# Retention of the first half in two blocks with a state between them, the state handed on as float32

## The chip, the cores and the metric

The kernel runs on one core of one Trainium2 chip. The metric is the device time of one execution in microseconds (us); before the change it is 1715.69 us, the median of three runs (1715.61, 1715.69 and 1717.03). The engines are named as in the profile: PE (TensorE, matmuls; PEld are its weight loads), DVE (VectorE), ACT (ScalarE), POOL (GpSimd) and SP (SyncE, which issues the DMAs).

## The reference

The reference is a trunk of two layers on 1024 tokens of width 1024. Layer 0 is retention with 4 heads (q and k of width 256, v of width 512), a norm of each head's output and a SiLU gate; layer 1 is stick-breaking attention with 8 heads on shared keys and values. Both are followed by an output projection, an RMS norm and the residual. What the change touches is retention:

```python
# o_t = sum_{s<=t} gamma_h^(t-s) (q_t . k_s) v_s
def step(state, inp):
    qc, kc, vc = inp
    scores = jnp.einsum('bhid,bhjd->bhij', qc, kc) * intra_decay
    o = jnp.einsum('bhij,bhje->bhie', scores, vc)
    o = o + jnp.einsum('bhid,bhde->bhie', qc * q_decay[None, :, :, None], state)
    state = state * chunk_decay[None, :, None, None] + jnp.einsum(
        'bhjd,bhje->bhde', kc * k_decay[None, :, :, None], vc)
    return state, o
```

The sum over earlier tokens can be cut anywhere: what lies in the same block goes through scores, what lies before it through a state of 256 x 512 numbers for each head.

## The kernel before, in words

The work has four phases: retention on the first 512 tokens (t=0), on the second 512 (t=1), then attention on each half. In a retention phase the four heads u = 0 to 3 follow each other. Each head has a projection of q and k (`qk`), one of v and the gate (`vg`), and an output projection (`out`, 16 chunks of 12 matmuls each), and the heads overlap: while the projections of head u run, `merge` strews in the steps of head u − 1 and u: the scores, the mixing of v (`mix`), the gate, and the norms of the neighbouring phase. A product is made in three matmuls (`mm3`: high with high at L415, high with low at L416, low with high at L417), because every float32 operand is kept as a high and a low part. `split` makes these: ACT writes the high part (L577), DVE the rest (L578).

Matmul results stand in PSUM banks under the tags "z" (scores, transposes, small sums), "o" (outputs of mix and states), "ma" and "mb" (projections). In the traces they are the tiles pz, po, pma and pmb; whl are split weights, xh split inputs, qk split q and k (and the last head's gated output), oT the gated output of other heads, ko split states, sc split scores, v split v, sgn normed outputs, wraw raw weights from memory.

At t=0 a head's scores are four steps `score(jb)`, the key block jb against all queries from there on (512, 384, 256 and 128 columns), and four `kt(tb)`, which transpose k. `o(ib)` then sums the score blocks 0 to ib times v. The state that the second half needs is made by two `state_out` steps, each a sum over all four token blocks; they lie beside the output projection (`L.give`), are scaled by a power of gamma, split, and written to memory as high and low parts (512 KB each). At t=1 `state_in` loads those parts as they are, and `o(ib)` takes the state's product and all score blocks.

The order around this is not written out by hand alone. `run` fixes which steps are strewn beside which projection (`nmix` says how many steps of mix lie beside `vg`; `held` is the output projection of the head before, of which a part goes in front of `vg` of the last head and the rest behind it). Then `arrange` takes the whole program and gives every engine's queue a new order by estimated costs, bank releases and due times. Within a queue the order is then fixed, so an instruction whose input isn't ready holds up everything behind it on that engine.

The last phase ends in `finish`: sums of squares, the mean over channels by matmuls with one column (L1454, L1455), a power on POOL (L1458), its broadcast by PE (L1464), the multiply by DVE (L1470) and the addition of the residual (L1471), then the DMA to the output.

Of the kernel before, what the change touches and what calls it, by code (L numbers as in the profile page):

```python
# [21 lines left out]
NH = 4  # L22
# [78 lines left out]
def arrange(nc, tc, tag_of, bufs, banks, turns):  # L101
# [4 lines left out]
    for ins in nc.cur_bb.bb.instructions:  # L106
# [12 lines left out]
        for name, m in reads:  # L119
            s.before |= {o.k for o, n, w in last[name] if w and n & m}  # L120
            s.behind |= set([o.k for o, n, w in last[name] if not w and n & m and o.eng == s.eng][-1:])
# [187 lines left out]
def trunk(ctx, tc, xT, wts, gains, trig, ident_in, cols, out):  # L309
# [26 lines left out]
    def DRAM(name, dt):  # L336
        return dr.tile([128, 1024], dt, tag=name, name=name)
# [15 lines left out]
    def hl(tag):  # L353
        return S(tag, [2, 512], F32R)
# [231 lines left out]

    st_d = [[DRAM(f"st{h}{d}", F32R) for d in range(2)] for h in range(NH)]
    y_d = [[dr.tile([128, 512], F32, tag=f"y{t}{c}", name=f"y{t}{c}") for c in range(8)] for t in range(2)]
# [137 lines left out]
    class AHead:  # L726
# [142 lines left out]
        def scores(self):  # L869
# [25 lines left out]

            st = [lambda jb=jb: score(jb) for jb in range(4)]
            if self.t == 0:
                st += [lambda tb=tb: kt(tb) for tb in range(4)]
            return st

        def mix(self):
# [3 lines left out]

            def state_out(d):
                p = PS("o")
                for tb in range(4):
                    n, kn, v = slice(128 * d, 128 * d + 128), self.kn[tb], self.v[tb]
                    mm3(p[:], kn[:, 0, n], kn[:, 1, n], v[:, 0, :], v[:, 1, :], tb == 0, tb == 3)  # L910
                s = hl("ko")
                gg = GAMMA[h] ** HT
                A_.activation(s[:, 0, :], p[:], AF.Copy, scale=gg)
                V.scalar_tensor_tensor(s[:, 1, :], p[:], gg, f32(s[:, 0, :]), ALU.mult, ALU.subtract)
                dma(st_d[h][d][:], flat(s))

            def state_in():
                for d in range(2):
                    s = hl("ko")
                    dma(flat(s), st_d[h][d][:])  # L920
                    self.state.append(s)

            def o(ib):
                p = PS("o")
                il = slice(128 * ib, 128 * ib + 128)
                for d, s in enumerate(self.state):
                    mm3(p[:], q[d][:, 0, il], q[d][:, 1, il], s[:, 0, :], s[:, 1, :], d == 0, False)
                for jb in range(ib + 1):
                    n = slice(128 * (ib - jb), 128 * (ib - jb) + 128)
                    sc, v = self.sc[jb], self.v[jb]  # L930
                    mm3(p[:], sc[:, 0, n], sc[:, 1, n], v[:, 0, :], v[:, 1, :], not self.state and jb == 0, jb == ib)
                bs, mv = S("small", [6]), S("small", [2])
# [480 lines left out]
    def finish(t, P, y_d):  # L1413
# [36 lines left out]
        def col(th):  # L1450
            p = PS("z")
            for b in range(2):
                o = 256 * th + 128 * b
                MM(p[:, b:b + 1], acc[:, o:o + 128], mean[:, 0:1], start=True, stop=False)  # L1454
                MM(p[:, b:b + 1], box["q"][:, 128 * b:128 * b + 128], mean[:, 0:1], start=False, stop=True)  # L1455
            ms, r = S("small", [2]), S("col", [4])
            V.tensor_scalar(ms[:], p[:, 0:2], EPS, None, ALU.add)
            G.tensor_tensor(r[:, 0:2], ms[:], mhalf[:, 0:2], ALU.pow)  # L1458
            box["r"] = r
# [6 lines left out]
        def write(th, k):  # L1466
            tl = slice(256 * th, 256 * th + 256)
            yy = f[:, 2 * k:2 * k + 2, tl]
            h = hs[k][:].rearrange("p (c t) -> p c t", c=2)[:, :, tl]
            V.tensor_tensor(yy, yy, box["row"][:, :256].unsqueeze(1).broadcast_to([128, 2, 256]), ALU.mult)  # L1470
            (G if th == 0 or k == 0 else V).tensor_tensor(yy, yy, h, ALU.add)  # L1471
            dma(out[256 * k:256 * k + 256, HT * t + 256 * th:HT * t + 256 * th + 256].rearrange("(c p) t -> p c t", c=2), yy)
# [20 lines left out]
    def run():  # L1493
# [12 lines left out]
        for ip, (kind, t) in enumerate(phases):  # L1506
# [5 lines left out]
            for u in range(4):  # L1512
                ring[:] = rings(kind, t, u)
                if kind == "A":
# [143 lines left out]
```

## Time and profile before

| | us |
|---|---|
| median of three runs | 1715.69 |
| the profiled execution | 1716.91 |
| its span | 1714.8 |
| PE busy | 1700.1 |
| DVE busy | 1308.4 |
| ACT busy | 880.9 |
| POOL busy | 142.8 |

The profile shows one execution. Its span runs from the first to the last instruction on the chip; the 2.1 us between it and the execution's time lie around it. "Busy" is the time in which at least one instruction was under way. Matmuls are pipelined, one starts before the last has ended, so their durations must not be added up: the distance between the starts of two is what one costs. A wait is shown behind an instruction in square brackets, with the time that its engine stood idle and the instruction that released it.

### The profile page before, as it was taken

To read this page: it belongs to the slowest core of one execution; us is meant where nothing else is said; L and a number is where in the kernel's file an instruction comes from. 1 tells how busy PE (TensorE), PEld (TensorE's weight loads), DVE (VectorE), ACT (ScalarE), POOL (GpSimd) and SP (SyncE) were. 2 spreads that over 40 slices of the span, in tenths; PEclk is the share of its full clock that TensorE was granted. 3 is DMA by queue.
4 is the path that set the end of the run, shared out by engine and by line. 5 is a ranking of instruction groups with operands and counts; after the bars stand their busy time and mean duration, and the time that the engine had idled before them with its cause. 6 is when DMAs were issued, how large, how long until landed. Compare 5 with 4: busy or idle time off the path is not lost.

```text
span 1714.8 us, 23975 instructions
## 1 busy us (share of the span) xinstructions
PE 1700.1 (99%) x8057; PEld 1419.0 (83%) x8057; DVE 1308.4 (76%) x2213; ACT 880.9 (51%) x1646; POOL 142.8 (8%) x275
## 2 busy tenths in 40 slices
PE   9999999999999999999999999999999999999997
PEld 7888888888888888878888888888888888888887
DVE  8856868889867978688888778667887756656865
ACT  6435536555545535355655544544674445445643
POOL 0000101010010000101010100000001001001001
PEclk9999999999999999999999999999999999999999
DMA  5236475668545676376896999667883763463523
GB/s 187 98 105 203 148 236 185 203 193 271 187 146 176 225 240 209 98 256 209 291 320 198 332 314 308 209 209 257 280 292 111 252 225 101 160 219 99 162 95 125
DMA packets 182250, 348.78 MB, mean 203 GB/s; under 512 B 20208, under 2 KB 24432, under 8 KB 182128
## 3 DMA queue, kind: packets, MB, share of 16 engines
q1 hardware_dynamic: 182128, 347.26, 61.0%
q8 instruction: 63, 1.03, 0.2%
q14 instruction: 59, 0.48, 0.1%
HBM read 273.78 MB, written 73.40 MB: 202 GB/s over the span
## 4 chain that ended last, share of the span: by engine, by line
PE 99%; DMA 0%; DVE 0%; ACT 0%; issue 0%; SPq 0%; POOL 0%; DVEq 0%
PE pmb L415 13%; PE pmb L417 13%; PE pmb L416 13%; PE pma L415 12%; PE pma L417 12%; PE pma L416 12%; PE po L417 5%; PE po L416 5%; PE po L415 5%; PE pz L1355 2%; PE pz L417 2%; PE pz L416 2%; PE pz L415 2%; PE pz L983 1%; PE pz L551 0%; DMA S<-in_xT_dram 0%
## 5 line engine op out<-in xcount | busy, mean ns | idle before, releaser
L577 ACT ACTIVATE whl<-wraw 128x512 fp32r<-128x512 f32 x323 | 190.8, 625 | 203.4 <-PE pmb L417 80.4
L578 DVE TENSOR_TENSOR whl<-wraw,whl 128x512 fp32r<-128x512 f32 x323 | 214.3, 686 | 64.3 <-ACT whl L577 63.1
L415 PE MATMUL pma<-xh,whl 128*128 128x512 f32 x384 | 153.1, 399 | 0.0
L415 PE MATMUL pmb<-xh,whl 128*128 128x512 f32 x384 | 152.4, 397 | 0.0
L417 PE MATMUL pma<-xh,whl 128*128 128x512 f32 x384 | 150.1, 391 | 0.0
L417 PE MATMUL pmb<-xh,whl 128*128 128x512 f32 x384 | 150.0, 391 | 0.0
L416 PE MATMUL pma<-xh,whl 128*128 128x512 f32 x384 | 149.9, 390 | 0.0
L416 PE MATMUL pmb<-xh,whl 128*128 128x512 f32 x384 | 149.6, 390 | 0.0
L1325 DVE TENSOR_TENSOR_SCAN sgn<-sgn 128x384 f32<-128x384 f32 (+4 forms) x64 | 86.5, 1354 | 27.7 <-POOL sgn L1323 27.7
L580 ACT ACTIVATE whl<-wraw,gn 128x256 fp32r<-128x256 f32 (+1 forms) x144 | 80.4, 600 | 50.0 <-PE pmb L417 32.4
L577 ACT ACTIVATE AT<-pz 128x512 fp32r<-128x512 f32 (+1 forms) x96 | 46.3, 487 | 108.0 <-PE pz L1355 105.9
L1322 POOL TENSOR_SCALAR_AFFINE_SELECT A<-A 128x128 f32<-128x128 f32 x64 | 33.1, 516 | 775.1 <-ACT A L1317 775.1
L578 DVE TENSOR_TENSOR AT<-pz,AT 128x512 fp32r<-128x512 f32 (+1 forms) x96 | 52.9, 555 | 57.6 <-ACT AT L577 57.1
L581 DVE SCALAR_TENSOR_TENSOR whl<-wraw,gn,whl 128x256 fp32r<-128x256 f32 (+1 forms) x144 | 82.0, 601 | 17.1 <-ACT whl L580 16.5
L415 PE MATMUL pmb<-oT,whl 128*128 128x512 f32 x240 | 94.9, 396 | 0.0
L417 PE MATMUL pmb<-oT,whl 128*128 128x512 f32 x240 | 93.8, 391 | 0.0
L416 PE MATMUL pmb<-oT,whl 128*128 128x512 f32 x240 | 93.7, 391 | 0.0
L577 ACT ACTIVATE whl<-S 128x512 fp32r<-128x512 f32 x104 | 63.0, 628 | 48.1 <-PE pmb L417 12.5
L417 PEld LDWEIGHTS pmb<-xh,whl 128*128 128x128 f32 x384 | 72.1, 188 | 15.8
L417 PEld LDWEIGHTS pma<-xh,whl 128*128 128x128 f32 x384 | 72.1, 188 | 15.6
L416 PEld LDWEIGHTS pmb<-xh,whl 128*128 128x128 f32 x384 | 72.2, 188 | 13.5
L415 PEld LDWEIGHTS pmb<-xh,whl 128*128 128x128 f32 x384 | 72.2, 188 | 13.4
(389 smaller groups left out, 4614.0 us busy)
## 6 DMA issues: line engine op xcount, KB each, us to landing
wraw<-in_wts_dram SPq DMA_DIRECT2D x522, 256.0 KB, 3.6
y<-f SPq DMA_DIRECT2D x120, 256.0 KB, 3.2
f<-y SPq DMA_DIRECT2D x88, 256.0 KB, 4.1
S<-in_wts_dram SPq DMA_DIRECT2D x44, 256.0 KB, 4.1
vo<-in_wts_dram SPq DMA_DIRECT2D x42, 256.0 KB, 4.3
ko<-in_wts_dram SPq DMA_DIRECT2D x40, 256.0 KB, 4.4
T<-AT SPq DMA_DIRECT2D x32, 256.0 KB, 4.7
sc<-T SPq DMA_DIRECT2D x16, 512.0 KB, 5.1
```

The costliest lines, as they stand in the source:

```text
L415: MM(p, lh, rh, start=start, stop=False, **kw)
L416: MM(p, lh, rl, start=False, stop=False, **kw)
L417: MM(p, ll, rh, start=False, stop=stop, **kw)
L577: A_.activation(dst[0], src, AF.Copy)
L578: V.tensor_tensor(dst[1], src, f32(dst[0]), ALU.subtract)
L580: A_.activation(dst[0], src, AF.Copy, scale=scale)
L581: V.scalar_tensor_tensor(dst[1], src, scale, f32(dst[0]), ALU.mult, ALU.subtract)
L983: nc.tensor.transpose(pt[:, 128 * e:128 * e + 128], on[:, 128 * e:128 * e + 128], ident[:])
L1322: first = G.affine_select(a[:, dg], a[:, dg], [[-1, 128]], ALU.is_gt, 0.0, base=0, channel_multiplier=1)
L1325: V.tensor_tensor_scan(n[:, :W][:, ::-1], n[:, :W][:, ::-1], n[:, :W][:, ::-1], 1.0, ALU.mult, ALU.bypass)
L1355: nc.tensor.transpose(p[:, 128 * tb:128 * tb + 128], self.A[hh][tb][:, c0:c0 + 128], ident[:])
```

## The change

Retention at t=0 is cut into two blocks of 256 tokens. For each head:

- the scores are two steps `pair(c)`, each with 256 and 128 columns in one bank, behind the transposes of k;
- `o(0)` and `o(1)` take the blocks 0 and 1, `o(2)` and `o(3)` take the state of the first block and the blocks 2 and 3;
- two `carry(d)` steps behind `o(0)` make the state: the first six matmuls sum the first 256 tokens, that sum is split (the state for `o(2)` and `o(3)`), and six more add the next 256 tokens in the same bank. ACT scales the result into a float32 tile "sc2", of which there is one buffer, and it is written as it is (256 KB). `state_out` and its place beside the output projection are gone;
- at t=1 `state_in` loads the float32 state into the ring of raw weights and splits it there.

Beside that, five steps of mix in place of two lie beside `vg` at t=0. Of the last head's held output projection eight chunks in place of four stand in front of `vg`, in banks of both tags. `arrange` now also puts a read of a PSUM tile behind earlier reads of it by another engine. In `finish` the four mean matmuls are reordered, for the second 256 tokens ACT copies half of two residual tiles into PSUM banks, and the additions are shared otherwise: POOL adds three of four for the first 256 tokens (four before) and two of four for the second (one before), DVE the others.

```diff
-            s.before |= {o.k for o, n, w in last[name] if w and n & m}
+            s.before |= {o.k for o, n, w in last[name] if n & m and (w or name in banks and o.eng != s.eng)}
...
-    st_d = [[DRAM(f"st{h}{d}", F32R) for d in range(2)] for h in range(NH)]
+    st_d = [[dr.tile([128, 512], F32, tag=f"st{h}{d}", name=f"st{h}{d}") for d in range(2)] for h in range(NH)]
...
-            st = [lambda jb=jb: score(jb) for jb in range(4)]
+            def pair(c):
+                p = PS("z")
+                for jb, at, w in ((2 * c, 0, 256), (2 * c + 1, 256, 128)):
+                    i0 = 256 * c + 256 - w
+                    jl, il = slice(128 * jb, 128 * jb + 128), slice(i0, i0 + w)
+                    for d in range(2):
+                        mm3(p[:, at:at + w], k[d][:, 0, jl], k[d][:, 1, jl], q[d][:, 0, il], q[d][:, 1, il],
+                            at == 0 and d == 0, at > 0 and d == 1, goes_on=True)
+                s = S(f"sc{c}", [2, 384], F32R)
+                split((s[:, 0, :], s[:, 1, :]), p[:, :384])
...
             if self.t == 0:
-                st += [lambda tb=tb: kt(tb) for tb in range(4)]
-            return st
+                return [lambda tb=tb: kt(tb) for tb in range(4)] + [lambda c=c: pair(c) for c in range(2)]
+            return [lambda jb=jb: score(jb) for jb in range(4)]
...
-            def state_out(d):
-                p = PS("o")
-                for tb in range(4):
-                    n, kn, v = slice(128 * d, 128 * d + 128), self.kn[tb], self.v[tb]
-                    mm3(p[:], kn[:, 0, n], kn[:, 1, n], v[:, 0, :], v[:, 1, :], tb == 0, tb == 3)
-                s = hl("ko")
-                gg = GAMMA[h] ** HT
-                A_.activation(s[:, 0, :], p[:], AF.Copy, scale=gg)
-                V.scalar_tensor_tensor(s[:, 1, :], p[:], gg, f32(s[:, 0, :]), ALU.mult, ALU.subtract)
-                dma(st_d[h][d][:], flat(s))
+            def carry(d):
+                p, gg, n = PS("o"), GAMMA[h] ** HT, slice(128 * d, 128 * d + 128)
+                for half in range(2):
+                    for tb in (2 * half, 2 * half + 1):
+                        kn, v = self.kn[tb], self.v[tb]
+                        mm3(p[:], kn[:, 0, n], kn[:, 1, n], v[:, 0, :], v[:, 1, :], tb == 0, tb % 2 == 1, goes_on=half == 1)
+                    if half == 0:
+                        s = hl("ko")
+                        split((s[:, 0, :], s[:, 1, :]), p[:])
+                        self.state.append(s)
+                f = S("sc2", [512])
+                A_.activation(f[:], p[:], AF.Copy, scale=gg)
+                dma(st_d[h][d][:], f[:])
...
-                    s = hl("ko")
-                    dma(flat(s), st_d[h][d][:])
+                    raw, s = raw_w(), hl("ko")
+                    dma(raw, st_d[h][d][:])
+                    split((s[:, 0, :], s[:, 1, :]), raw)
...
-                for d, s in enumerate(self.state):
+                j0 = 0 if self.t else ib // 2 * 2
+                far = self.state if self.t or j0 else []
+                for d, s in enumerate(far):
...
-                for jb in range(ib + 1):
+                for jb in range(j0, ib + 1):
...
-            if self.t == 0:
-                self.give = [lambda d=d: state_out(d) for d in range(2)]
-                return os
             self.give = []
-            return [state_in] + os
+            if self.t:
+                return [state_in] + os
+            return os[:1] + [lambda d=d: carry(d) for d in range(2)] + os[1:]
...
-            (G if th == 0 or k == 0 else V).tensor_tensor(yy, yy, h, ALU.add)
+            if th and k > 1:
+                h = box[k][:].rearrange("p (c t) -> p c t", c=2)
+            (G if k < (2 if th else 3) else V).tensor_tensor(yy, yy, h, ALU.add)
...
-                        held = last.out(yd, None, None if u < 3 else ("ma",) * 4)
-                        go(held if u < 3 else held[:4],
+                        held = last.out(yd)
+                        go(held if u < 3 else held[:8],
...
-                        held = held[4:]
-                    H.nmix = 3 if t else 2
+                        held = held[8:]
+                    H.nmix = 3 if t else 5
```

In the rows below, a row is an instruction of one engine's queue, with the engines and queues that it waits for in brackets (Activation is ACT).

The first place is PE's queue where `vg` of the last head at t=1 begins. The L569 pair sums up rows for the next phase's norm, pz<-qk are the head's scores, pma and pmb<-oT the held chunks, pma<-whl,xh the projection. Before:

```order
L417 MATMUL pma_7094<-oT_6787,whl_7011 128x512
L569 MATMUL pz_7111<-sgn_7067,onesr 128x512 [waits DVE_49,PE_49]
L569 MATMUL pz_7111<-sgn_7067,onesr 128x512 [waits DVE_49]
L415 MATMUL pz_7187<-qk_6988 128x512 [waits PE_49,Activation_49]
L416 MATMUL pz_7187<-qk_6988 128x512 [waits DVE_49]
```

And now:

```order
L417 MATMUL pmb_7139<-oT_6789,whl_7069 128x512
L569 MATMUL pz_7156<-sgn_7095,onesr 128x512 [waits DVE_49,PE_49]
L569 MATMUL pz_7156<-sgn_7095,onesr 128x512 [waits DVE_49]
L415 MATMUL pma_7170<-whl_7121,xh_3856 128x512 [waits DVE_49,Activation_49]
L416 MATMUL pma_7170<-whl_7121,xh_3856 128x512
```

The first score matmul of the head now stands 36 matmuls behind the pair, and the projection's first product stands in its place.

The second place is PE's queue at the end of the last head's gate at t=1: pz<-ident are the transposes of the gate (L983 before, L1003 now), pmb<-oT the end of the held chunks, pma<-qk the first chunk of this head's own output projection, which reads what the transposes leave. Before, the transposes and the first reader, with 24 matmuls between them:

```order
L417 MATMUL pma_7734<-oT_6787,whl_7624 128x512
L983 MATMUL pz_7760<-ident,sgn_7672 128x128 [waits DVE_49,PE_49]
L983 MATMUL pz_7760<-ident,sgn_7672 128x128 x3
L415 MATMUL pmb_7767<-oT_6787,whl_7725 128x512
```

```order
L417 MATMUL pmb_7797<-oT_6787,whl_7725 128x512
L415 MATMUL pma_7815<-qk_7578,whl_7788 128x512 [waits Activation_49]
L416 MATMUL pma_7815<-qk_7578,whl_7788 128x512 [waits DVE_49]
```

And now:

```order
L416 MATMUL pmb_7805<-oT_6789,whl_7713 128x512
L1003 MATMUL pz_7765<-ident,sgn_7705 128x128 [waits DVE_49,PE_49]
L1003 MATMUL pz_7765<-ident,sgn_7705 128x128 x3
L417 MATMUL pmb_7805<-oT_6789,whl_7713 128x512
L415 MATMUL pma_7823<-qk_7629,whl_7796 128x512 [waits Activation_49]
L416 MATMUL pma_7823<-qk_7629,whl_7796 128x512 [waits DVE_49]
```

One matmul is left between the transposes and the reader.

The third place is PE's queue in the first head's first carry at t=0. po_942 is the carry's bank, v_403 and vo_734 its first operands, pmb and pma the projection beside it. Before, the state's twelve matmuls stood together, with no wait among them, beside the output projection. Now:

```order
L417 MATMUL po_942<-v_406,vo_765 128x512
L415 MATMUL pmb_898<-xh_434,whl_832 128x512
L416 MATMUL pmb_898<-xh_434,whl_832 128x512
L417 MATMUL pmb_898<-xh_434,whl_832 128x512
L415 MATMUL pmb_899<-xh_434,whl_832 128x512
L416 MATMUL pmb_899<-xh_434,whl_832 128x512
L417 MATMUL pmb_899<-xh_434,whl_832 128x512
L415 MATMUL pma_896<-xh_463,whl_927 128x512
L416 MATMUL pma_896<-xh_463,whl_927 128x512
L415 MATMUL po_942<-v_427,vo_799 128x512 [waits DVE_49]
```

Eight matmuls of the projection stand between the two halves, and the second half waits for DVE, which must have read the first half's sums.

More of the change, by code (lines that the diff above doesn't have):

```diff
@@ L894, in score @@
                 self.sc.append(s)
-            st = [lambda jb=jb: score(jb) for jb in range(4)]
+            def pair(c):
[8 more added lines that the diff above has]
+                split((s[:, 0, :], s[:, 1, :]), p[:, :384])
+                for at in (0, 256):
+                    G.affine_select(s[:, :, at:at + 128], f32(s[:, :, at:at + 128]), [[0, 2], [1, 128]], ALU.is_ge, 0.0,
+                                    base=0, channel_multiplier=-1)
+                self.sc += [s[:, :, 0:256], s[:, :, 256:384]]
             if self.t == 0:
-                st += [lambda tb=tb: kt(tb) for tb in range(4)]
-            return st
+                return [lambda tb=tb: kt(tb) for tb in range(4)] + [lambda c=c: pair(c) for c in range(2)]
+            return [lambda jb=jb: score(jb) for jb in range(4)]
         def mix(self):
@@ L925, in o @@
                 il = slice(128 * ib, 128 * ib + 128)
-                for d, s in enumerate(self.state):
+                j0 = 0 if self.t else ib // 2 * 2
+                far = self.state if self.t or j0 else []
+                for d, s in enumerate(far):
                     mm3(p[:], q[d][:, 0, il], q[d][:, 1, il], s[:, 0, :], s[:, 1, :], d == 0, False)
-                for jb in range(ib + 1):
+                for jb in range(j0, ib + 1):
                     n = slice(128 * (ib - jb), 128 * (ib - jb) + 128)
                     sc, v = self.sc[jb], self.v[jb]
-                    mm3(p[:], sc[:, 0, n], sc[:, 1, n], v[:, 0, :], v[:, 1, :], not self.state and jb == 0, jb == ib)
+                    mm3(p[:], sc[:, 0, n], sc[:, 1, n], v[:, 0, :], v[:, 1, :], not far and jb == j0, jb == ib)
                 bs, mv = S("small", [6]), S("small", [2])
@@ L1453, in col @@
                 o = 256 * th + 128 * b
-                MM(p[:, b:b + 1], acc[:, o:o + 128], mean[:, 0:1], start=True, stop=False)
-                MM(p[:, b:b + 1], box["q"][:, 128 * b:128 * b + 128], mean[:, 0:1], start=False, stop=True)
+                MM(p[:, b:b + 1], acc[:, o:o + 128], mean[:, 0:1], start=b == 0, stop=False, skip_group_check=True)
+            for b in range(2):
+                MM(p[:, b:b + 1], box["q"][:, 128 * b:128 * b + 128], mean[:, 0:1], start=False, stop=b == 1, skip_group_check=True)
+            if th:
+                for k in (2, 3):
+                    box[k] = PS("ma")
+                    A_.activation(box[k][:].rearrange("p (c t) -> p c t", c=2),
+                                  hs[k][:].rearrange("p (c t) -> p c t", c=2)[:, :, 256:512], AF.Copy)
             ms, r = S("small", [2]), S("col", [4])
```

## The prediction

> **What bounds the kernel now.** I read the page's first lines, then the chain that ended last, then PE's own waits, then the busy time by stretches.
>
> ```profile
> span 1714.8 us, 23975 instructions
> PE 1700.1 (99%) x8057; PEld 1419.0 (83%) x8057; DVE 1308.4 (76%) x2213; ACT 880.9 (51%) x1646; POOL 142.8 (8%) x275
> PE 99%; DMA 0%; DVE 0%; ACT 0%; issue 0%; SPq 0%; POOL 0%; DVEq 0%
> ...
> PE pz L415 <- ACT qk L577: 1.8, 1, 1.8
> PE pz L1464 <- POOL col L1458: 1.0, 1, 1.0
> PE pz L1454 <- DVE acc L1447: 0.9, 1, 0.9
> ...
> 385.83:428.70 42.87, 42.87 (x197) 35.49 (x196) 41.44 (x75) 22.15 (x40) 0.00 (x0) 1.00 0.82 271
> 728.79:771.66 42.87, 41.05 (x180) 33.74 (x179) 37.41 (x62) 24.00 (x44) 1.94 (x3) 0.96 0.78 257
> 1671.93:1714.80 42.87, 33.09 (x255) 31.76 (x253) 23.24 (x49) 16.32 (x36) 8.27 (x7) 0.91 0.38 125
> ```
>
> PE is busy 99% of the span and carries 99% of the chain, so the time is the sum of PE's paces, plus its few waits, plus the end. A saving on another engine counts only where PE waits. There are three such places here: one wait of 1.8 us for a split (in 728.79 to 771.66, where PE is busy 41.05 of 42.87 us and the granted clock is 0.96), two of about 1 us at the end, and the end itself, which is work of DVE and POOL. The other danger is a stretch like 385.83 to 428.70: there DVE is busy 41.44 of 42.87 us while PE is full.
>
> The profiled run took 1716.91 us, 2.1 over its span, and 1.2 over the median of 1715.69 us. I sum against 1716.91 and keep the 1.2 for the low end of the range.
>
> **Part 1: narrower scores.** The matmuls of each o(ib) keep their number and width (3, 6, 9, 12), and the state's matmuls were there before, 24 a head. What goes is width in the scores of four heads: per head 6 matmuls each of 512, 384, 256 and 128 columns become twice 6 of 256 and 6 of 128. Durations overlap, so a matmul's price is the distance between starts.
>
> ```profile
> 64.22 0.39 PE L415 MATMUL pz<-qk 128*128 128x512 f32 x1
> 65.58 0.39 PE L415 MATMUL pma<-whl,xh 128*128 128x512 f32 x1
> 66.94 0.33 PE L415 MATMUL pz<-qk 128*128 128x384 f32 x1
> 68.00 0.39 PE L415 MATMUL pma<-whl,xh 128*128 128x512 f32 x1
> 69.39 0.28 PE L415 MATMUL pz<-qk 128*128 128x256 f32 x1
> 70.10 0.39 PE L415 MATMUL pmb<-whl,xh 128*128 128x512 f32 x1
> 71.48 0.22 PE L415 MATMUL pz<-qk 128*128 128x128 f32 x1
> 72.10 0.44 PE L415 MATMUL pmb<-whl,xh 128*128 128x512 f32 x1
> 72.39 0.40 PE L416 MATMUL pmb<-whl,xh 128*128 128x512 f32 x1
> ```
>
> Each block is timed to the first start behind it: 1.36 us (65.58 − 64.22), 1.06, 0.71 and 0.62. The wide matmul behind the narrowest ones took 0.29 (72.39 − 72.10) in place of 0.227 (1.36/6), so 0.06 more. A head's scores cost 3.81 us; afterwards 2 × (0.71 + 0.62 + 0.06) = 2.78. Times four heads this is **−4.1 us**, all on PE, so all on the path. The pace follows width down to 0.10 us a matmul in these rows (0.62/6), so nothing else caps it; I allow 0.4 either way.
>
> **Part 2: the wait at 730.** Where the last head of the second half begins, its first score matmul waited for the split of q and k (L577).
>
> ```profile
> 729.88 0.63 PE L569 MATMUL pz<-sgn,onesr 128*128 128x512 f32 x2
> 732.33 0.50 PE L415 MATMUL pz<-qk 128*128 128x512 f32 x1 [1.82 <-ACT qk L577]
> 735.77 0.63 PE L415 MATMUL pma<-whl,xh 128*128 128x512 f32 x1
> 736.20 0.63 PE L416 MATMUL pma<-whl,xh 128*128 128x512 f32 x1
> 737.45 0.40 PE L416 MATMUL pma<-whl,xh 128*128 128x512 f32 x1
> 737.68 0.39 PE L417 MATMUL pma<-whl,xh 128*128 128x512 f32 x1
> ```
>
> Two matmuls of 0.227 from 729.88 end their pace at 730.33, so the start at 732.33 is 2.00 us late. Then the clock is low: 735.77 to 736.20 is 0.43 us for a matmul that takes 0.23 at 737.45. From 732.33 to 737.45 stand 6 matmuls of 512, 5 of 384 and 4 of 512; at normal pace that is 10 × 0.227 + 5 × 0.177 = 3.15 us, and it took 5.12, so 1.97 more. Together 4.0 us. Afterwards eight held chunks of the out-projection go first instead of four, and 36 matmuls (8.2 us) of the value and gate projection stand between the pair of L569 and the first score. That covers the 1.8 us four times over, so I take **−4.0 us**. What becomes next late is the split of the first weights of that projection. They are loaded by the same ring, and the added four chunks (48 matmuls, 10.9 us) give their splits room; I count 1 to 4 us to spare for the first three. Bounds: −4.0, and 0 if the wait only moves to those weights.
>
> [...]
>
> **Part 3: the end.** The last writes are DVE's multiplies (L1470), then adds (L1471).
>
> ```profile
> 1707.03 2.48 DVE L1470 TENSOR_TENSOR oT<-oT,pz 128x512 f32<-128x512 f32 x4 [1.63 <-PE pz L1464]
> 1707.86 1.27 POOL L1471 TENSOR_TENSOR oT<-oT,A 128x512 f32<-128x512 f32 x1 [1.67 <-DVE oT L1470]
> 1709.43 1.89 DVE L1471 TENSOR_TENSOR oT<-oT,A 128x512 f32<-128x512 f32 x3
> ```
>
> DVE adds three times at 0.63 us; afterwards twice, and POOL's second add (1.27) follows its first at 1709.13 and ends at 1710.4, before DVE's second (1710.7). So **−0.6 us**. The two copies on ACT fall while the mean and its power are worked out, where ACT has nothing else. The first half's add that moves to DVE costs 0.6 if it delays the last sums, and the reordered mean matmuls can give back as much: bounds 0 to −1.2.
>
> **Part 4: the new wait at the last head's gate.** This is the price of the eight chunks. Only eight remain to cover the gate of head 3 in the second half, so its last transposes stand one matmul ahead of the first reader of qk; 24 stood there before.
>
> ```profile
> 800.84 0.60 PE L983 MATMUL pz<-ident,sgn 128*128 128x128 f32 x4
> 801.20 0.48 PE L415 MATMUL pmb<-oT,whl 128*128 128x512 f32 x1
> 801.64 0.58 ACT L577 ACTIVATE qk<-pz 128x512 fp32r<-128x512 f32 x1
> 802.25 0.69 DVE L578 TENSOR_TENSOR qk<-pz,qk 128x512 fp32r<-128x512 f32 x1
> 806.76 0.39 PE L415 MATMUL pma<-qk,whl 128*128 128x512 f32 x1
> ```
>
> The split ends at 802.94 (802.25 + 0.69). With one matmul behind the transposes and one of the reader's that needs only ACT's part, PE would be through at 801.20 + 0.46 = 801.66: a gap of 1.3 us. ACT was late by about 0.2 for a weight split of 801.10, which need not stand there. I take **+1.1 us**, bounds 0 (if the transposes come through early) and 1.3, and 2.0 more if the clock drops as after 732.33. In the first half's last gate six matmuls (1.4 us) remain, about as long as the split; there I count nothing, and 0.2 if it is late.
>
> **Part 5: the carries.** Each of eight carries now stops half way: its second six matmuls overwrite the sums that ACT and DVE are splitting. Between the halves stand 8 to 12 other matmuls, 1.8 to 2.7 us, and a prompt split takes 0.2 (801.64 after the transposes' end at 801.44) + 0.60 + 0.68 = 1.5. So I count nothing; the cover is 0.3 to 1.2 us thick, and each place costs what the queue of ACT or DVE holds beyond it. The scaled copy into the one "sc2" buffer makes the second carry's copy wait for the first one's DMA, 20 matmuls (4.5 us) later, and its bank is wanted another 30 (6.8 us) after that. The DMA now carries 256 KB; 512 KB took 5.5 us in the median, so nothing is counted either.
>
> ```profile
> st<-ko SPq DMA_DIRECT2D x8, 512.0 KB, 5.5
> ```
>
> The split of the loaded state (eight operations of 0.6 us on ACT and eight on DVE) lies beside full PE work, far ahead of its readers.
>
> **Sum.** 1716.91 − 4.1 − 4.0 − 0.6 + 1.1 = **1709.3 us**, 6.4 under the median, 0.37%.
>
> **The rivals.**
>
> Slower: the splits between the carry's halves come late. Before, the two halves of the same kind of split stood far apart on their engines.
>
> ```profile
> 325.71 0.60 ACT L913 ACTIVATE ko<-po 128x512 fp32r<-128x512 f32 x1 [0.99 <-PE po L417]
> 326.58 0.68 DVE L914 SCALAR_TENSOR_TENSOR ko<-po,ko 128x512 fp32r<-128x512 f32 x1
> 401.22 0.60 ACT L913 ACTIVATE ko<-po 128x512 fp32r<-128x512 f32 x1 [1.72 <-PE po L417]
> 420.67 0.68 DVE L914 SCALAR_TENSOR_TENSOR ko<-po,ko 128x512 fp32r<-128x512 f32 x1
> ```
>
> At 325.71 DVE followed ACT by 0.87 us, at 401.22 by 19.5. With that lag in the last head's two carries PE would wait about 2 × (19.5 + 0.9 − 2.7) = 35 us: 1744. It decides from 1.4 us a place (11 us over eight places eats the gains of 7.6 and 3.4 more). Against it: nobody waited for the split then, so DVE took it last; now it stands in DVE's queue right behind the sums it reads, and by DVE's paces I find it done 0.3 to 1 us early. Chance 4%.
>
> DVE bounds the passage from the first to the second half. Held chunks and state matmuls (10.9 us of PE) leave the stretch before head 0 of the second half, where DVE was full, and DVE's work there stays.
>
> ```profile
> 415.12 0.42 DVE L636 TENSOR_TENSOR f<-S 128x256 f32<-128x256 f32 x1
> 415.46 0.68 DVE L517 TENSOR_TENSOR f<-pma,f 128x512 f32<-128x512 f32 x1
> 416.06 0.41 DVE L637 TENSOR_TENSOR f<-S,f 128x256 f32<-128x256 f32 x1
> ```
>
> DVE's pace is 0.34 us for 256 columns and 0.60 for 512. From the last o(3) to the weights of that head's third unit I count 41 wide operations, 11 half-wide, 4 of the norm (0.66 each) and 0.8 us of small ones: 31.9 us, plus 1.2 of waiting at the gate. PE has 147 matmuls and four sets of transposes there, 35.0 us. It holds by 1.9 us. If it fails it costs 2 to 6 us with the clock: 1711.3 to 1715.3. Chance 9%, half of it above 1712.3.
>
> The clock drops after part 4's wait: +2.0, 1711.3, chance 10%. The row at 732.33 speaks for it, its wait was longer.
>
> The slow stretch at 732 was not the wait's, and only 2.0 of part 2 come back: 1711.3. For it: two other waits at the end were not followed by wide matmuls, so the rows show it once only. Chance 8%. [...]
>
> The wait at 730 moves whole to the first weights: 1713.3, chance 4%.
>
> **How the numbers follow.** The forecast has 65%. About 0.2% (3.4 us, so 1712.3) is what a measurement of this kernel can tell from no change. Faster: 65 + 10 + 8 + half of 9 is 87%. Same: 5 + 4 is 9%. Slower: 4%. The low end is 1709.3 − 1.2 (the median against the profiled run) − 1.1 (no wait at the gate) − 0.6 (the end) − 0.4 (the scores) = 1706.0; the high end is the wait that moves whole, 1713.3. Left out are the slower rival and the upper half of DVE's, some 9%.
>
> **What would show it.** Scores of 256 and 128 columns in one bank, 1.39 us a pair; no wait of PE for qk behind L569, and a granted clock of 1.00 there; a wait of about 1 us of the matmul pma<-qk on the split behind the last gate; two adds of DVE at the end, 0.6 us earlier. Wrong would be: waits of po on DVE inside the carries, PE below full in the passage from the first to the second half, or a new low clock anywhere.

## The result, and the profile after

The changed kernel takes 1709.84 us in the median of six runs (1708.51 to 1710.98), the kernel before 1715.65 (1715.2 to 1717.25, six runs). The ratio is 0.9963, with a 95% interval from 0.9953 to 0.9973: 5.8 us faster, 0.37%. The prediction was 1709.3 us, in a range from 1706.0 to 1713.3.

The profiled run took 1709.47 us with a span of 1707.8. First lines of the page, PE's waits (who waited for whom: total, times, longest), and three stretches of it (length, then busy time of PE, PEld, DVE, ACT and POOL, then granted clock, DMA share, GB/s):

```profile
span 1707.8 us, 23993 instructions
PE 1694.7 (99%) x8057; PEld 1414.8 (83%) x8057; DVE 1309.3 (77%) x2213; ACT 888.2 (52%) x1656; POOL 141.9 (8%) x275
...
PE pz L1490 <- POOL col L1484: 1.0, 1, 1.0
PE pmb L416 <- DVE whl L578: 0.7, 1, 0.7
PE pma L415 <- ACT qk L577: 0.5, 1, 0.5
PE pz L1474 <- DVE acc L1467: 0.3, 1, 0.3
PE pma L416 <- DVE qk L578: 0.2, 1, 0.2
...
384.25:426.95 42.70, 42.70 (x198) 35.27 (x197) 40.22 (x75) 21.90 (x39) 1.01 (x3) 1.00 0.76 259
725.82:768.51 42.69, 42.69 (x196) 35.58 (x195) 38.45 (x65) 25.01 (x45) 5.14 (x2) 1.00 0.87 289
768.51:811.21 42.70, 42.01 (x192) 34.35 (x191) 38.13 (x67) 22.02 (x40) 8.54 (x14) 1.00 0.64 206
```

PE is still busy 99% of the span. The wait for qk of 1.8 us is gone, and in the stretch 725.82 to 768.51 PE is full at a granted clock of 1.00. New is a wait for qk in 768.51 to 811.21 (0.5 and 0.2 us, the reader behind the last gate) and one for whl of 0.7. The passage to the second half (384.25 to 426.95) is full: DVE did not become the bound there. The wait of the mean matmuls fell from 0.9 to 0.3 us, and a wait of 1.2 us for oT in the first 10 us is not there. That one is not the change's: in three more profiles of the kernel before (below) such waits are 1.5, 0.3 and 1.2 us together.

The scores of one pair, in PE's timeline of the changed kernel (start, length, instruction):

```profile
74.52 0.28 PE L415 MATMUL pz<-qk 128*128 128x256 f32 x1
75.23 0.22 PE L415 MATMUL pz<-qk 128*128 128x128 f32 x1
75.85 0.45 PE L415 MATMUL pmb<-whl,xh 128*128 128x512 f32 x1
76.14 0.39 PE L416 MATMUL pmb<-whl,xh 128*128 128x512 f32 x1
```

From 74.52 to 75.85 are 1.33 us, and the wide matmul behind takes 0.29 in place of 0.23: 1.39 us a pair, the predicted figure to the digit, so 2.78 us a head in place of 3.81. Counted in the same way over all four heads, the scores take 15.2 us of PE before and 11.1 after.

The gate of the last head, PE, ACT and DVE of the changed kernel:

```profile
797.84 0.60 PE L1003 MATMUL pz<-ident,sgn 128*128 128x128 f32 x4
798.20 0.47 PE L417 MATMUL pmb<-oT,whl 128*128 128x512 f32 x1
798.48 0.60 ACT L577 ACTIVATE qk<-pz 128x512 fp32r<-128x512 f32 x1 [1.81 <-PE pz L1003]
799.11 0.69 DVE L578 TENSOR_TENSOR qk<-pz,qk 128x512 fp32r<-128x512 f32 x1
799.13 0.49 PE L415 MATMUL pma<-qk,whl 128*128 128x512 f32 x1 [0.46 <-ACT qk L577]
799.85 0.50 PE L416 MATMUL pma<-qk,whl 128*128 128x512 f32 x1 [0.23 <-DVE qk L578]
```

The reader starts 0.70 us later than a matmul's pace behind 798.20, and its second matmul 0.49 later still: 1.2 us, against 1.1 predicted. The end:

```profile
1697.34 0.61 PE L1476 MATMUL pz<-mean,f 128*128 128x1 f32 x4
1699.73 2.48 DVE L1496 TENSOR_TENSOR oT<-oT,pz 128x512 f32<-128x512 f32 x4 [1.59 <-PE pz L1490]
1700.56 2.50 POOL L1499 TENSOR_TENSOR oT<-oT,A 128x512 f32<-128x512 f32 x2 [1.63 <-DVE oT L1496]
1702.12 1.28 DVE L1499 TENSOR_TENSOR oT<-oT,pma 128x512 f32<-128x512 f32 x2
```

DVE adds twice and is done at 1703.40, POOL at 1703.06, as forecast.

The two profiled spans differ by 7.0 us. From the starts of PE's matmuls: scores −4.1; the wait at 730 and the slow matmuls behind it −4.0; the gate +1.2; a later split of whl near 560 +0.7; waits in the first 20 us about −0.8; and the end, from the start of the last projection matmul to the span's end, −0.1 (11.84 before, 11.77 after). Together −7.1.

### The profile page after: what moved, and what is told of

Same layout as the page of the kernel before. It is cut to its first block, busy times and chain, and to the rows that moved or that the text cites. A ratio compares the mean times of both kernels' runs of the same rounds, so it can differ in the third digit from the quotient of the medians.

```text
span 1707.8 us, 23993 instructions
## 1 busy us (share of the span) xinstructions
PE 1694.7 (99%) x8057; PEld 1414.8 (83%) x8057; DVE 1309.3 (77%) x2213; ACT 888.2 (52%) x1656; POOL 141.9 (8%) x275
## 4 chain that ended last, share of the span: by engine, by line
PE 96%; DVE 2%; DMA 1%; issue 0%; ACT 0%; SPq 0%; POOL 0%; DVEq 0%
PE pmb L415 13%; PE pmb L417 12%; PE pmb L416 12%; PE pma L415 12%; PE pma L416 12%; PE pma L417 12%; PE po L417 5%; PE po L416 5%; PE po L415 5%; PE pz L1375 2%; PE pz L417 1%; PE pz L416 1%; PE pz L415 1%; PE pz L1003 1%; DMA ko<-in_xT_dram 0%; PE pz L551 0%
## 5 line engine op out<-in xcount | busy, mean ns | idle before, releaser
L415 PE MATMUL pmb<-oT,whl 128*128 128x512 f32 x256 | 101.3, 396 | 0.0
L416 PE MATMUL pmb<-oT,whl 128*128 128x512 f32 x256 | 100.1, 391 | 0.0
L417 PE MATMUL pmb<-oT,whl 128*128 128x512 f32 x256 | 100.1, 391 | 0.0
```

Source lines behind the costliest of these rows:

```text
L415: MM(p, lh, rh, start=start, stop=False, **kw)
L416: MM(p, lh, rl, start=False, stop=False, **kw)
L417: MM(p, ll, rh, start=False, stop=stop, **kw)
```

## The experiments

Each kernel is timed in runs of its own; the median is compared with 1709.84 of the changed kernel, whose runs spread over 2.5 us. The kernel of before, timed beside the experiments in three groups, had medians of 1715.48, 1716.04 and 1716.15 (1715.65 beside the changed kernel), so differences of about 0.5 us between kernels of different groups are not to be trusted. Where a cause is named, the profile of that kernel shows it.

**undo_held**: the held chunks as before the change, the rest as changed.

```diff
-                        held = last.out(yd)
-                        go(held if u < 3 else held[:8],
+                        held = last.out(yd, None, None if u < 3 else ("ma",) * 4)
+                        go(held if u < 3 else held[:4],
...
-                        held = held[8:]
+                        held = held[4:]
```

> The changed kernel with four held chunks in front of the last head's projection, as before, all in one bank tag. Theory: the wait of the first score matmul behind the L569 pair at t=1 comes back (about 1.8 us, followed by some 5 us of slow matmuls, 4.0 us together), and the wait of 1.2 us behind the last gate goes: +2.8 us on 1709.84, so about 1712.6. Rival 1 (the slow matmuls were not the wait's): a wait of about 2 us and no slow matmuls behind it, +0.8, so 1710.6. Rival 2 (the wait had come from the state matmuls beside the output projection, which are gone): no wait there at all, -1.2, so 1708.6.

Measured: 1717.04 us (1714.46 to 1718.38), 7.2 us slower than the changed kernel and 1.0009 of the kernel before (1.0000 to 1.0018). All three expectations missed. PE's waits in its profile:

```profile
PE pma L415 <- DVE f L517: 3.7, 1, 3.7
PE pz L415 <- ACT qk L577: 1.8, 1, 1.8
PE pz L388 <- DVE f L386: 1.7, 1, 1.7
PE pz L1490 <- POOL col L1484: 1.0, 1, 1.0
```

The wait for qk is back, as expected, and the one behind the gate is gone. But there is also a wait of 3.7 us that neither the kernel before nor the changed one has. It stands near 320, in the first half.

**ret_only**: the kernel of before with the retention alone.

```diff
-                        go(held if u < 3 else held[:8],
+                        go(held if u < 3 else held[:4],
...
-            (G if k < (2 if th else 3) else V).tensor_tensor(yy, yy, h, ALU.add)
+            (G if th == 0 or k == 0 else V).tensor_tensor(yy, yy, h, ALU.add)
```

(From the changed kernel, shortened: all of the held chunks and of `finish` is as before.)

> The kernel of before with the retention in two blocks alone (scores, carry, loaded state, steps of mix, the rule on reads); held chunks and the end as before. Theory: the narrower scores alone, -4.1 us, and the wait at the last head's first score stays with its slow matmuls: 1715.65 - 4.1 = 1711.6; by the other two undone parts, 1709.84 + 2.8 + 0.6 = 1713.2, so between 1711.6 and 1713.2. Rival: the carries and the loaded state cost something that another part hides, so the scores' gain is under 2 us: over 1713.6.

Measured: 1717.84 us (1715.88 to 1719.85), 1.0014 of the kernel before (1.0005 to 1.0022): the retention alone is slower. The rival's time was met, but not for its reason: PE waits nowhere for a carry (po) or a loaded state. Its timeline of PE near 320 (a bracket is the wait before the instruction, and what ended it):

```profile
322.12 0.95 PE L551 MATMUL pz<-ones,acc 128*128 128x1 f32 x8
326.78 0.50 PE L415 MATMUL pma<-whl,xh 128*128 128x512 f32 x1 [3.71 <-DVE f L517]
327.46 0.63 PE L417 MATMUL pma<-whl,xh 128*128 128x512 f32 x1
327.88 0.63 PE L415 MATMUL pma<-whl,xh 128*128 128x512 f32 x1
```

and DVE's in the same kernel, part of it:

```profile
322.00 0.67 DVE L720 TENSOR_TENSOR f<-pmb,tab 128x512 f32<-128x512 f32 x1
323.11 0.16 DVE L553 TENSOR_SCALAR small<-pz 128x4 f32<-128x4 f32 x1 [0.43 <-PE pz L551]
326.05 0.68 DVE L517 TENSOR_TENSOR f<-pma,f 128x512 f32<-128x512 f32 x1
```

The projection of the last head wants the bank pma, and DVE reads the held chunk out of it (L517) only at 326.05, behind the rotary work on q and k (L717 to L722). Matmuls then start 0.42 us apart (327.46 to 327.88), so the wait costs 5.5 us. With the scores (−4.1) and waits of 1.6 us for the split of whl near 560 that makes +3.0, and this profiled run is 2.9 us above that of the kernel before. In the kernel before, PE at the same place (last head at t=0):

```profile
314.63 0.39 PE L415 MATMUL pma<-oT,whl 128*128 128x512 f32 x1
317.35 0.39 PE L415 MATMUL po<-v,vo 128*128 128x512 f32 x1
320.07 0.39 PE L415 MATMUL pma<-oT,whl 128*128 128x512 f32 x1
322.79 0.39 PE L415 MATMUL po<-v,vo 128*128 128x512 f32 x1
326.32 0.49 PE L415 MATMUL pma<-whl,xh 128*128 128x512 f32 x1
```

and DVE's first L517 there:

```profile
323.31 0.68 DVE L517 TENSOR_TENSOR f<-pma,f 128x512 f32<-128x512 f32 x1
```

There the two state products (po<-v,vo, 12 matmuls or 2.7 us each) lay between the held chunks, and DVE reached L517 in time. Counted from the first held matmul (314.63 before, 316.68 in ret_only), DVE begins L517 after 8.7 us before and 9.4 in ret_only; PE is ready for the projection after 11.7 us before, and in ret_only, without the wait, after 6.3 (322.12 and 0.81 for the eight small matmuls). So DVE is nearly where it was, and PE comes 5.4 us sooner: the carries took these 5.4 us of PE work away to another place.

**t0_4** and **t1_4**: four held chunks in one half only, eight in the other.

```diff
-                        held = last.out(yd)
-                        go(held if u < 3 else held[:8],
+                        held = last.out(yd, None, None if u < 3 else (("ma",) * 4, None)[t])
+                        go(held if u < 3 else held[:(4, 8)[t]],
...
-                        held = held[8:]
+                        held = held[(4, 8)[t]:]
```

(t1_4: the pairs the other way round.)

> The changed kernel with four held chunks in front of the last head's projection at t=0 alone (in one bank tag, as before the change), eight at t=1. Theory (new since undo_held and ret_only: the two state products had lain between these chunks and covered DVE's rotary work, and with them gone the next projection waits for a bank that DVE still has to read): a wait of about 3.7 us for DVE's L517 near 320 and 1.7 us of slow matmuls behind it, nothing at 730, the wait behind the last gate as it is: +5.5, so 1715.3. Rival (the wait near 320 comes from the chunks' bank tag or from chance): under 1711.5.

> The changed kernel with four held chunks at t=1 alone (in one bank tag), eight at t=0. Theory: the wait of 1.8 us at the last head's first score is back, with 0.5 to 2.0 us of slow matmuls behind it (two profiles showed 0.5 and 2.0), the one behind the last gate is gone, and nothing happens near 320: +2.3 to +4.0 - 1.2, so 1710.9 to 1712.6. With t0_4 it should add up to what undo_held lost, 7.2 us. Rival: the two phases hang together and the parts do not add up: outside 6 to 9 us.

Measured: t0_4 1714.83 us (1714.25 to 1717.32), 5.0 slower than the changed kernel; t1_4 1711.12 (1709.6 to 1712.8), 1.3 slower. Of the two waits of undo_held, t0_4 has the one for L517 and not the one of 1.8 us for qk:

```profile
321.67 0.95 PE L551 MATMUL pz<-ones,acc 128*128 128x1 f32 x8
326.33 0.79 PE L415 MATMUL pma<-whl,xh 128*128 128x512 f32 x1 [3.71 <-DVE f L517]
```

In t1_4 it is the other way round. Together they lose 6.3 us, undo_held 7.2: with medians that are good to about 0.5 us, the halves add up. So the eight chunks are worth 5.0 us in the first half, where they replace the cover of the state products, and 1.3 in the second, where they remove an old wait and add the one behind the gate.

**t0_ma**: all eight chunks of t=0 in the banks of the tag ma, in place of both tags.

```diff
-                        held = last.out(yd)
+                        held = last.out(yd, None, ("ma",) * 4 if u == 3 and t == 0 else None)
```

> The changed kernel with all eight held chunks of t=0 in the two banks of one tag (ma), which the next projection also wants first; the number of matmuls ahead of it is as in the changed kernel. What is open: whether near 320 the 24 added matmuls count as time in which DVE catches up, or the other two banks that they use. Theory 1 (time): the wait of 3.7 us stays away or is under 1 us, and the time is 1709.8 to 1711. Theory 2 (banks): the projection waits for DVE's last additions out of ma as in t0_4, 2 us or more with slow matmuls, and the time is 1712 or more.

Measured: 1711.67 us (1710.42 to 1714.4), between the two expectations. PE waited 1.8 us for L517, now at the third of the four held sums and not at the projection:

```profile
324.64 0.51 PE L415 MATMUL pma<-oT,whl 128*128 128x512 f32 x1 [1.83 <-DVE f L517]
```

Of the 5.0 us, then, about 1.8 hang on the two other banks and 3.2 on the time of the added matmuls, to about 0.5 us.

**held6**: six held chunks in front in both halves, ten behind.

```diff
-                        go(held if u < 3 else held[:8],
+                        go(held if u < 3 else held[:6],
...
-                        held = held[8:]
+                        held = held[6:]
```

> The changed kernel with six held chunks in front of the last head's projection and ten behind it. In PE's queue twelve matmuls then stand between the last gate's transposes and the first reader (one in the changed kernel), and the first score stands right behind the L569 pair again, as before the change. Theory (cover by time: two chunks more are 5.4 us for a wait of 1.8): no wait at the scores and none at the gate: -1.2, so 1708.6. Rival (the score's place in the queue decides, since ACT and DVE are queued behind the same chunks): a wait of 1 to 2 us at the scores with slow matmuls, +1 to +2.8, so 1710.8 to 1712.6.

Measured: 1712.79 us (1712.04 to 1714.93), 3.0 slower: the rival, and 0.2 over the top of its range. Its waits:

```profile
PE pma L415 <- DVE f L517: 1.4, 2, 1.1
PE pz L415 <- ACT qk L577: 1.4, 1, 1.4
```

The gate's wait is gone, as both expected, but the wait for qk shrank only from 1.8 to 1.4, and part of the one for L517 is back, 1.1 us of it in the first half. A chunk has six matmuls, not twelve, so two chunks are 2.7 us and not the 5.4 of the expectation; but even 2.7 exceed 1.8. Where the first score stands in PE's queue, right behind the L569 pair, decided more than the matmuls ahead of it.

**nmix5**: the last head's mix at t=1 wholly beside its projection.

```diff
-                    H.nmix = 3 if t else 5
+                    H.nmix = (5 if u == 3 else 3) if t else 5
```

> The changed kernel with the last head's mix at t=1 put wholly beside its projection (five steps in place of three, so the last o and its norm no longer wait for the held chunks). In PE's queue eleven matmuls then stand between the last gate's transposes and the first reader, one in the changed kernel; the first score stands as in the changed kernel. Theory: the wait of 1.2 us behind the gate goes and nothing takes its place: 1708.6. Rival: the outputs now wait for DVE or ACT inside the projection, where more is queued: 1709.8 or more.

Measured: 1708.91 us (1707.95 to 1709.55), 0.9 faster than the changed kernel and 0.9959 of the kernel before (0.9945 to 0.9973; the changed kernel had 0.9963, from 0.9953 to 0.9973). Rows of the same place as above:

```profile
797.72 0.68 DVE L578 TENSOR_TENSOR qk<-pz,qk 128x512 fp32r<-128x512 f32 x1
797.77 0.40 PE L416 MATMUL pmb<-oT,whl 128*128 128x512 f32 x1
798.70 0.39 PE L417 MATMUL pmb<-oT,whl 128*128 128x512 f32 x1
798.92 0.39 PE L415 MATMUL pma<-qk,whl 128*128 128x512 f32 x1
```

The split is over at 798.40 (797.72 + 0.68) and the reader starts at 798.92 without a wait. So the wait is gone, as the theory said. The median is the lowest of the study, but the two intervals overlap, and that it is faster than the changed kernel is not shown by the times alone.

**undo_fin**: the end (mean matmuls, additions) as before the change.

```diff
-            if th and k > 1:
-                h = box[k][:].rearrange("p (c t) -> p c t", c=2)
-            (G if k < (2 if th else 3) else V).tensor_tensor(yy, yy, h, ALU.add)
+            (G if th == 0 or k == 0 else V).tensor_tensor(yy, yy, h, ALU.add)
```

(Shortened: the order of the mean matmuls is the old one too, and the two copies on ACT are gone.)

> The changed kernel with the end (mean matmuls, additions) as before. Theory: DVE's last addition ends 0.6 us later counted from the last projection matmul (8.4 us in place of 7.4 to 7.8), time +0.6, so about 1710.4. Rival: the landing of the output DMAs hides it, as in the one profile of the changed kernel, in which the distance from the last projection matmul to the span's end was 11.8 us before and after: 1709.8, no difference.

Measured: 1710.35 us (1709.45 to 1711.62), 0.5 slower, near the 0.6 but within the spread. From the start of the last projection matmul to the span's end it is 12.2 us in the mean of six profiles with the old end (11.84 to 12.70) and 11.9 in eight with the new (11.66 to 12.35). DVE's last addition does end earlier, at 7.4 to 7.9 us behind that matmul in place of 8.4 to 8.8: 0.6 from the addition, the rest from the mean matmuls, whose wait fell from 0.9 to 0.3. But most of this is lost again behind it, where 4.3 to 4.5 us pass to the span's end in place of 3.4 to 3.9. In the changed kernel the last addition is done at 1703.40, and SP issues its DMA at 1703.86, behind the issue for POOL's (1703.30, 0.47 us long); in the kernel before it was issued 0.07 us behind the last addition. So 0.3 to 0.5 us is what can be said, and the times alone don't show even that.

**no_edge**: without the rule that orders reads of a PSUM tile by different engines.

```diff
-            s.before |= {o.k for o, n, w in last[name] if n & m and (w or name in banks and o.eng != s.eng)}
+            s.before |= {o.k for o, n, w in last[name] if w and n & m}
```

> The changed kernel without the rule that a read of a PSUM tile comes behind earlier reads of it by another engine. Theory: the carries had cover to spare, no wait of po appears, and the time stays at 1709.8 within 0.8. Rival: DVE's half of a split is then taken late, the carries' second halves wait, and the time is over 1712.

Measured: 1711.98 us (1709.77 to 1712.57), 2.1 slower, at the rival's edge; the theory missed, since a wait of po is there. One carry waits (DVE's half of its split starts 2.3 us behind ACT's, 0.6 in the changed kernel), and the gate waits longer:

```profile
PE po L415 <- DVE ko L578: 0.9, 1, 0.9
PE pma L415 <- ACT qk L577: 0.8, 1, 0.8
...
PE pma L416 <- DVE qk L578: 0.3, 1, 0.3
```

So this line of the change, to which the prediction gave no price, is worth up to 2 us; the profile accounts for 1.5 of them (1.1 at the carry, 0.4 more at the gate). The wait for whl near 560, whose cause is open (below), is 0.5 longer as well.

**before_b, before_c, before_d**: the kernel of before, unchanged, profiled three more times.

> The kernel of before, unchanged, for another profile. What is open: the prediction gave 2.0 us to the slow matmuls behind the wait at the last head's first score; after the same wait of 1.82 us two profiles (before, ret_only) showed 2.0 us of excess in the next 10 us, two (undo_held, t1_4) 0.5. Theory 1 (it belongs to the kernel): 2.0 again. Theory 2 (it changes from run to run): 0.5 in some of these profiles, and then a span about 1.5 us shorter.

> The kernel of before, unchanged, for a third profile: as before_b.

> The kernel of before, unchanged, for a fourth profile: as before_b.

The busy times and granted clock (the figure of 0.91 or 1.00) from 725 to 745, first of the profile before, then of before_b:

```profile
725.00:745.00 20.00, 18.18 (x74) 14.57 (x73) 15.86 (x29) 9.43 (x17) 1.21 (x2) 0.91 0.53 172
```

```profile
725.00:745.00 20.00, 18.18 (x80) 14.52 (x79) 16.55 (x30) 10.61 (x19) 0.82 (x2) 1.00 0.63 188
```

The wait is 1.82 us in all four profiles. Behind it the matmuls lose 2.0 us in two (before, before_d; clock 0.91) and 0.5 in two (before_b, before_c; clock 1.00). It changes from run to run. Read in a narrower stretch, the low clock of the profile before is one slow block:

```profile
734.00:737.40 3.40, 3.40 (x11) 2.99 (x10) 3.21 (x6) 0.60 (x1) 0.12 (x1) 0.50 0.87 287
```

By the trace's records of the clock the block is 3.41 us long, at half speed, in before and in before_d, and it is absent in before_b and before_c: that is 1.7 us. The other 0.3 to 0.5 us are in all four: the first three matmuls behind the wait start 0.33 to 0.39 us apart in place of 0.23, while the clock is still 1.00. These profiles also show the waits for oT in the first 10 us at 1.5, 0.3 and 1.2 us together, so the 0.8 us there can't be put down to the change.

## Why the prediction was right

**The sum.** Predicted −7.6 us against the profiled run, measured −7.4 (1716.91 to 1709.47); against the median −6.4 and −5.8. The difference between these two pairs is mostly the clock below: the profiled run of before had the slow block of 1.7 us, which two of its four profiles lack.

**Scores, −4.1: right.** A pair took 1.39 us, as worked out. Over the four heads it is 15.2 to 11.1 us. This part is measured on the matmuls themselves.

**The wait at 730, −4.0: right in kind, one half mis-sized.** The first score no longer waits, and undoing the eight chunks at t=1 brings exactly this wait back (t1_4). But of the 4.0 only the wait of 2.0 is there in every run; the slow matmuls cost 0.5 or 2.0. I had priced them from the one profile that had the larger figure. Against a run without the slow block the term is −2.5; the run to start from is then lower by the same 1.5 us, so the forecast of the time does not move, but that of the gain does. The rival that the slow matmuls were "not the wait's" is not borne out: seven profiles have this wait of 1.8, in each the first matmuls right behind it are slow, the slow block stands behind it in three of them, and between the first 8 us of a kernel and its end no such block stands anywhere but at a wait. The changed kernel has neither. The block followed four of the eight waits of 1.8 us, and one of 1.1 us too (held6). By the trace's records of the clock, full clock stood for 727.04 us ahead of the block of before and for 969.39 us behind it, 213 and 284 times the block's length of 3.413 us; no run shows what sets when it comes.

**The room for the weights was miscounted.** I wrote that the four added chunks are 48 matmuls and 10.9 us, and the description above gives a chunk twelve. A chunk is half a sum, six matmuls; the four are 24, 5.4 us. So the 1 to 4 us that I counted to spare for the first weights rested on twice the room there is; PE did not wait for them. The cover of the score itself, 36 matmuls of the projection, was counted rightly, and held6 bears it out: with two chunks more but the score right behind the L569 pair, 1.4 of the 1.8 us stay.

**The gate, +1.1: right.** It measured 1.2, without a drop in the clock; nmix5 takes it away, with a median lower by 0.9, within the spread.

**The end, −0.6: right on DVE, too large at the span's end.** DVE adds twice and ends about 1 us earlier, more than forecast, but the last DMA is issued behind the one for POOL's second addition, and 0.1 (the two profiles) to 0.5 us (the medians, within the spread) are left. The bounds of 0 to −1.2 hold.

**The step that was missing.** The prediction said that the state's matmuls were there before, and priced their move at nothing but a danger for DVE in the passage to the second half. It did not ask what they had covered where they stood. They covered 5 us: without the eight chunks at t=0 a wait of 3.7 us opens (t0_4), and the retention alone makes the kernel slower (ret_only). I gave the eight chunks credit for the wait at 730 alone. That the sum came out right all the same was luck: one edit of the change pays for a loss of another, and both fell out of my account.

**The other rivals.** At each of the eight carries DVE's half of the split followed ACT's within 0.63 us, and nobody waited for it; the first of them (ACT, then DVE, then the second half on PE, in the changed kernel):

```profile
84.98 0.60 ACT L577 ACTIVATE ko<-po 128x512 fp32r<-128x512 f32 x1 [5.49 <-PE po L417]
85.61 0.69 DVE L578 TENSOR_TENSOR ko<-po,ko 128x512 fp32r<-128x512 f32 x1 [2.25 <-ACT ko L577]
86.60 0.39 PE L415 MATMUL po<-v,vo 128*128 128x512 f32 x1
```

The split ends at 86.30, 0.3 us before PE comes; over the eight it is 0.3 to 0.8, the cover that the prediction counted. That this is thin shows in no_edge, where one carry waits 0.9. DVE as the bound at 388 to 428 did not come about.

**What stays open.** The split of whl near 560 is waited for by 0.5 to 1.4 us in several kernels (the changed one, undo_fin, t1_4, nmix5, no_edge, t0_ma, ret_only), by 0.2 in held6, and not at all in undo_held, t0_4 and the four profiles of before. In the changed kernel DVE takes a scaling of v between two of these splits, which before it did not; but it does so in undo_held and t0_4 too, where nobody waits. What differs there is how long DVE itself waited for the raw weights (L797, for a DMA) a few us ahead: 0.8 to 0.9 us in those two, 1.1 in held6, 1.3 to 2.6 in the others that wait (undo_fin has two such waits, 1.5 together). In the four profiles of before it is 0.4 to 1.5, and without the scaling nobody waits. Both may have a part; neither was tried alone, so which edit causes it is not settled. That five steps of mix in place of two lie beside `vg` at t=0 was not undone alone either.

## What to carry to other kernels

When matmuls are moved, ask what they covered where they stood, not only what they meet where they go: here 24 matmuls, taken from between two bank releases, cost 5.5 us there, more than the 4.1 us that the narrower scores save. An edit of order that looks like tuning may be what pays for another edit, so weigh the parts together and test them one at a time. A price read from one profile needs a second profile when it hangs on the clock: here the matmuls behind the same wait of 1.82 us lost 2.0 us in two profiles of the kernel before and 0.5 in two.

## What the runs showed of the hardware that was not expected

Behind waits of PE of 1.1 to 1.8 us the clock fell in some profiles and not in others, in the same program too: behind the wait of 1.82 us it fell in before and before_d and stayed at 1.00 in before_b and before_c. Where it fell, the granted clock was 0.50 for 3.41 us (6.83 in t0_4), beginning 0.1 to 1.7 us behind the wait's end (in t0_4 within the wait). It happened after all three waits of 3.7 us (undo_held, ret_only, t0_4), after four of eight of 1.8 us (before, before_d, ret_only, t0_ma), after one of 1.1 us (held6), and not after those of 1.4 us (ret_only, held6), 1.2 us (no_edge), 1.1 us (nmix5) and shorter ones. So in these runs the length of the wait alone did not decide; what else did, they don't show.

The excess of the matmuls in the 10 us behind a wait, over their usual pace (0.23 us between the starts of two with 512 columns), fell into two groups: 1.7 to 2.0 us with the slow block (2.7 in t0_4), 0.2 to 0.7 without it, most of that in the first matmuls behind the wait. So a wait of 1.1 us on a full TensorE cost 1.4 (nmix5) or 2.9 us (held6), and this is one source of the spread of the runs before.
